# Queries of branch A's heads 2 and 3 moved from the projection stage into the gate steps, as a ninth pair of seven half-size products

## The chip, the cores and the metric

The kernel runs on one core of one Trainium2 chip. The metric is the device time of one execution in microseconds; the kernel before takes 1424.58 us (median of three executions, 1423.66 to 1425.17). The engines named below are PE (TensorE, the matrix unit; PEld is its loading of the stationary operand), DVE (VectorE), ACT (ScalarE), POOL (GpSimd) and SP (SyncE, which here issues almost all DMA transfers). Each works through its own stream of instructions in order, and semaphores tie the streams together.

## What is computed

One encoder block over 1024 tokens of width 1024, with 16 meta tokens in front of them that are dropped from the output. All data is float32. Cut to what matters here:

```python
proj = rms_norm(h, norm_mix) @ w_in        # qa, ka, va, qb, kb, vb, ga, gb side by side
y_a = differential_attention(qa, ka, va)   # 4 heads, two score maps each, all keys
y_b = windowed_gqa(qb, kb, vb, sink)       # 8 heads on 2 key heads, window 128
merged = sigmoid(ga) * (y_a @ w_ba) + sigmoid(gb) * (y_b @ w_bb)
h = h + merged @ w_o
h = h + swiglu(rms_norm(h, norm_ffn))
out = rms_norm(h, norm_final)
```

In branch A the queries `qa` of one head are 128 columns of `w_in`: twice 64, for the two score maps. Heads 2 and 3 are columns 256 to 511, side by side. Of `qa`, `ga` and `gb` only the rows of the 1024 tokens are used.

## The kernel before

**Precision.** [...] Each operand is split into a high part (a cast) and a low part (what the cast left), and a product is made of three: high by high, high by low, low by high. So a product of 128 output columns by 512 tokens over a depth of 1024 is 8 x 3 matmuls of 128 x 512; over a depth of 512 it is 4 x 3.

**Stage one: projections and branch B.** The normed tokens lie transposed in SBUF as `hT_hi` and `hT_lo`. `project_steps` (lines 219 to 234) projects 128 columns at a time; `order` (lines 204 to 209) lists the columns in the order in which their weights are loaded and split. `project_qa(h)` (lines 643 to 649) makes the queries of head h of branch A in two chunks of 512 tokens, 24 matmuls each; `evac_split` scales, splits and stages them, and they go to `qa_d[h]` in DRAM, high and low part in turn, for both maps. `project_kva(h)` makes values and keys. `units_b(g, qb)` runs branch B's attention, group g, over eight tiles of 128 queries. A tile (`attend_b`, lines 382 to 444) is a chain: scores on PE for four heads (line 397), bias and minimum on DVE (399), exponentials on ACT (403, 405), sum and reciprocal on DVE (406, 407), scaling on POOL (409), a copy of the meta columns on POOL (413), transposes on PE (422, 432), splits on ACT and DVE (425, 428, 434, 435), values on PE (429, 437), output on ACT and DVE (440, 441), store on SP (442). Two tiles may be under way; their transposes share two PSUM banks and their scores two more. In this stage a scheduler that plays the program through before the run sets the order on each engine; the projections that follow in the program are drawn in between the steps of B. On POOL `tokens_mixed` makes the sums of token blocks that the gates need, and keeps them in `t_d`.

**Stage two: branch A with gate steps between.** From line 1074 on PE's order is written out by hand. Branch A's attention runs over four heads of eight tiles, 32 in all. A tile has four score pieces ("s": `scores_a`, lines 959 to 996, which begins by needing the head's `aq` and `ak`), three transposes of the tile before ("t"), three parts of values or of the norm of earlier tiles ("n"), and gate steps ("g") between them. `SLOTS` (line 41) gives this order for a tile, `SLOTS_LAST` for what follows the last. `load_a(h)` queues the loads of a head's queries and keys when its first tile begins, followed by six gate steps (`G_HEAD`), 24 for head 0 (`G_FIRST`); two more stand before tile 1.

**The gates.** The 2048 gate columns are eight pairs of two blocks of 128 columns. A pair is a 2 x 2 product over halves (two column blocks, two token halves, two halves of the depth), and it is made by Winograd's scheme with seven products of half depth instead of eight: numbers p = 1, 2, 6, 5, 7, 3, 4, each 12 matmuls of 128 x 512, in four steps of three matmuls. Where p takes a sum of token blocks, that sum is loaded over a quarter of `hT_hi` and `hT_lo` (`turn_into`, lines 811 to 825), once all products that need the quarter as it was are done. So the products of all pairs run in two phases: `first_g` (lines 732 to 734) lists p = 1, 2, 6 of the eight pairs, then follow p = 5, 7, 3, 4 pair by pair (line 735). Between the phases a partial sum of each pair waits in DRAM (`u_d`) and is loaded back into `kept[k]` one or two products ahead of its use, where ACT copies it into a PSUM bank (lines 857 to 864).

`weights_g(n)` (lines 761 to 800) makes the operand of product n on POOL: sums of weight blocks (lines 777 to 790), then a cast and a subtraction (799, 800). Raw weights come through four buffers (`load_g`, lines 747 to 757; `n_freed` counts the buffers given back); operands have four places. `gate_steps` (lines 827 to 920) issues the products and takes the results out through tiles of the tag "g", of which there are three, and of the tag "u", of which there are four. Stores are collected in `held_stores` and issued on SP after head 0's values are queued.

Of the 224 steps, the last 22 (`HOLD`) are kept out of the slots and run after the last tile. What follows (projection of both branches from line 1268, output projection, feed-forward part) is made in the same way for both kernels.

## Time and profile before

| | before |
|---|---|
| median of three executions | 1424.58 us |
| the profiled execution | 1424.24 us |
| its span, first to last instruction | 1421.9 us |
| granted TensorE clock, mean | 0.998 |
| PE busy | 1401.0 us, 99% of the span |
| DVE, ACT, POOL busy | 64%, 47%, 45% |
| matmuls | 7183 |
| chain that ended last: PE's share | 90% |

How to read the views. A group of instructions has its source line, engine, operation, the tile it writes and the tiles it reads. The busy time of PE holds the whole duration of each matmul, and neighbouring matmuls overlap; the chain of waits has each piece once, so its pieces give the distance at which matmuls follow each other. In the chain a row is: start in us, length in us, engine, tile, line, and how many instructions. A timeline row is the same with shapes, and at its end in brackets the idle time before it and what ended it. A window row is: window and its length, then busy time and number of instructions of PE, PEld, DVE, ACT and POOL, the granted clock, the share of time in which the DMA engines were busy, and GB/s. A row of waits is: who waited, for whom, us in total, how often, the longest.

### The profile page before, as it was taken

How to read it: one execution, taken by the hardware profiler on the slowest of the kernel's cores; microseconds unless marked ns; L12 is line 12 of the kernel's file. 1: busy time of each engine (PE TensorE's matmuls, PEld its weight loads, DVE VectorE, ACT ScalarE, POOL GpSimd, SP SyncE). 2: the span in 40 equal slices, each digit the busy share in tenths (PEclk: the TensorE clock that was granted, in tenths of full speed). 3: DMA queues.
4: the chain of work that ended last, by engine and by line, in shares of the span. 5: the costliest groups of instructions: out<-in, count | busy, mean ns of one | idle time of the engine just before them, and what ended most of it. 6: DMA issues, size and time to landing. Idle time of an engine off the chain costs nothing.

```text
span 1421.9 us, 20667 instructions
## 1 busy us (share of the span) xinstructions
PE 1401.0 (99%) x7183; PEld 1202.7 (85%) x7183; DVE 914.8 (64%) x1584; ACT 672.1 (47%) x1284; POOL 636.7 (45%) x648
## 2 busy tenths in 40 slices
PE   9999999998999999999999999999999999999998
PEld 8998999987888888878888888888888888888886
DVE  6555666527787878666978956544555453787566
ACT  6355556435445555455346644333333333444454
POOL 4156865546677666322503055555545441000442
PEclk9999999999999999999999999999999999999999
DMA  8446565386896363296522724433333323954343
GB/s 235 92 128 184 154 199 160 106 290 225 259 318 211 105 209 105 68 342 198 149 103 90 207 90 148 148 106 98 101 111 104 97 97 110 353 186 144 120 128 144
DMA packets 194297, 228.27 MB, mean 161 GB/s; under 512 B 16824, under 2 KB 127360, under 8 KB 194192
## 3 DMA queue, kind: packets, MB, share of 16 engines
q1 hardware_dynamic: 192272, 224.11, 49.3%
q10 hardware_dynamic: 1920, 2.83, 0.7%
q8 instruction: 57, 0.93, 0.3%
q14 instruction: 48, 0.39, 0.1%
HBM read 152.48 MB, written 67.86 MB: 155 GB/s over the span
## 4 chain that ended last, share of the span: by engine, by line
PE 90%; DVE 4%; DMA 2%; ACT 1%; issue 1%; SPq 1%; POOL 1%; ACTq 0%; POOLq 0%; DVEq 0%
PE pg L1634 29%; PE pd L1738 14%; PE pg L881 8%; PE ppa L721 6%; PE po L1537 4%; PE pp_va L230 3%; PE pp_ka L230 3%; PE aps L977 3%; PE pp_qa L230 3%; PE apy L1019 3%; PE pp_qb L230 3%; PE bps L397 2%; PE po L1545 2%; PE bpy L437 1%; PE apt L1006 1%; PE bpt L432 1%
## 5 line engine op out<-in xcount | busy, mean ns | idle before, releaser
L1634 PE MATMUL pg<-t,wop 128*128 128x512 f32 x1056 | 242.5, 389 | 0.0
L1634 PEld LDWEIGHTS pg<-t,wop 128*128 128x128 f32 x1056 | 198.3, 188 | 41.1
L120 POOL TENSOR_TENSOR wop<-wf,wop 128x512 fp32r<-128x512 f32 x114 | 153.9, 1351 | 162.4 <-ACT wop L119 148.7
L1738 PE MATMUL pd<-ob,oa 128*128 128x512 f32 x924 | 210.1, 390 | 0.2 <-DVE ob L120 0.2
L1738 PEld LDWEIGHTS pd<-ob,oa 128*128 128x128 f32 x924 | 173.4, 188 | 36.8 <-DVE ob L120 1.0
L1634 PE MATMUL pg<-b,wop 128*128 128x512 f32 x792 | 183.3, 390 | 0.0
L1634 PEld LDWEIGHTS pg<-b,wop 128*128 128x128 f32 x792 | 148.5, 188 | 30.7
L881 PE MATMUL pg<-hT_hi,wopg 128*128 128x512 f32 x448 | 169.9, 400 | 2.7 <-POOL wopg L800 1.8
L119 ACT ACTIVATE wop<-wf 128x512 fp32r<-128x512 f32 x128 | 80.8, 633 | 73.4 <-PE pg L1634 44.3
L120 POOL TENSOR_TENSOR oa<-ra,oa 128x512 fp32r<-128x512 f32 x27 | 34.9, 1294 | 169.4 <-ACT oa L119 167.7
L119 ACT ACTIVATE oa<-ra 128x512 fp32r<-128x512 f32 x77 | 48.7, 632 | 109.0 <-PE pd L1738 50.8
L988 ACT ACTIVATE as<-as,amn 128x1040 f32<-128x1040 f32 x64 | 74.5, 1165 | 50.6 <-DVE amn L984 50.4
L881 PEld LDWEIGHTS pg<-hT_hi,wopg 128*128 128x128 f32 x448 | 84.3, 188 | 15.5 <-POOL wopg L800 2.2
L1411 DVE TENSOR_TENSOR s<-wf,wf 128x512 f32<-128x512 f32 x22 | 17.6, 798 | 112.2 <-DMA wf<-in_w_ff_up_dram 70.7
L977 PE MATMUL aps<-ak,aq 128*128 128x352 f32 (+1 forms) x384 | 86.6, 334 | 2.4 <-DVE amn L980 2.2
L881 PE MATMUL pg<-hT_lo,wopg 128*128 128x512 f32 x224 | 88.2, 394 | 0.0
L980 DVE CUSTOM_DVE_ANT_0 as<-aps,dist,far_a 128x704 f32<-128x704 f32 x64 | 60.3, 943 | 34.9 <-PE aps L977 34.6
L399 DVE CUSTOM_DVE_ANT_0 bs<-bps,tbx,nsink 128x432 f32<-128x432 f32 (+1 forms) x64 | 38.6, 629 | 61.6 <-PE bps L397 37.8
L1009 ACT ACTIVATE at<-apt 128x512 fp32r<-128x512 f32 (+1 forms) x96 | 45.4, 484 | 63.0 <-PE apt L1006 63.0
L977 PEld LDWEIGHTS aps<-ak,aq 128*128 128x128 f32 x384 | 64.2, 189 | 12.2 <-DVE amn L980 4.7
L409 POOL TENSOR_SCALAR bs<-bs,bdn 128x432 f32<-128x432 f32 (+1 forms) x64 | 36.9, 596 | 75.3 <-DVE bdn L407 34.4
L1019 PEld LDWEIGHTS apy<-at,av 128*128 128x128 f32 x400 | 54.2, 190 | 4.0
(321 smaller groups left out, 3131.1 us busy)
## 6 DMA issues: line engine op xcount, KB each, us to landing
ra<-aop SPq DMA_DIRECT2D x77, 256.0 KB, 2.7
wf<-in_w_ff_gate_dram SPq DMA_DIRECT2D x25, 512.0 KB, 3.8
wf<-in_w_ff_up_dram SPq DMA_DIRECT2D x25, 512.0 KB, 3.8
aop<-as SPq DMA_DIRECT2D x44, 256.0 KB, 2.1
w_c<-in_w_in_dram SPq DMA_DIRECT2D x17, 512.0 KB, 4.8
aop<-c SPq DMA_DIRECT2D x33, 256.0 KB, 2.0
ak<-ka_d SPq DMA_DIRECT2D x16, 520.0 KB, 6.5
t_d<-tst SPq DMA_DIRECT2D x16, 512.0 KB, 3.8
```

What stands on the lines that cost most here:

```text
L119: high = nc.scalar.activation(hi, src, AF.Copy)
L120: lo_eng.tensor_tensor(lo, src, f32(hi), ALU.subtract)
L230: product = nc.tensor.matmul(ps[:, :n], a[:, c, :], b[:, c, at:at + n], start=(u == 0), stop=(u == 3 * DC - 1))
L721: nc.tensor.matmul(ps, w[:, a, j, :], src(j, b, tk), start=(j == 0 and n == 0), stop=(j == 3 and n == 2))
L881: nc.tensor.matmul(ps, op[:, x, c, :], h[:, 4 * d + c, HALF[t]], start=(p in (1, 6, 7) and c == 0 and i == 0), stop=(p in (2, 6, 3, 4) and ...
L977: nc.tensor.matmul(ps[:, :n], qs[m][:, t * P:(t + 1) * P], ks[m][:, vv, k0:k0 + n], start=(vv == 0), stop=(vv == 1))
L980: nc.vector.tensor_tensor_reduce(s[m][:, 0:2 * n].rearrange("p (a k) -> p a k", a=2), two[:, :, :n], dist[:, u0:u0 + 2 * n].rearrange("p ( ...
L988: nc.scalar.activation(s[m][:, 0:L], s[m][:, 0:L], AF.Exp, bias=mn[:, m, 1:2], scale=-1.0, accum_out=dn[:, 1:2] if m else first_sum)
L1019: nc.tensor.matmul(py[:, cols], v[:kp, a, k, :], at_[:kp, k, b, :], start=(k == 0 and j == 0), stop=(k == 8))
L1537: nc.tensor.matmul(sets_o[p][u], oa[:, a, u * P:(u + 1) * P], ob[:, b, :], start=(p in (1, 5) and j == 0 and k == 0), stop=(p in (2, 3) an ...
L1634: nc.tensor.matmul(ps, op[:, x, c, :], b[:, y, c, :], start=(p in (1, 5) and c == 0 and n == 0), stop=(p in (4, 2, 3) and c == 3 and n == ...
L1738: nc.tensor.matmul(ps[u], oa[:, a, u * P:(u + 1) * P], ob[:, b, :], start=(p in (1, 2, 5) and j == 0 and k == 0), stop=(p in (2, 3, 4) and ...
```

## The change

`project_qa` is no longer called for heads 2 and 3, and their columns leave the list of weights of stage one. Instead the columns 256 to 511 become a ninth pair, `Q_PAIR` = 8, of the gate scheme: its products 1, 6 and 2 stand in the first phase ahead of the last gate pair, and it is the first pair of the second phase. A new function `keep_q` takes its four finished blocks out of PSUM: ACT scales and casts, DVE makes the low part, and four stores of 64 x 512 each go to `qa_d`. One block of `u_d` is added for its partial sum. The gate steps become 63 x 4 = 252 instead of 224. `SLOTS` becomes three strings: tiles of heads 0 and 1 alternate between one with six and one with seven gate steps, heads 2 and 3 keep five.

```diff
-SLOTS = "ssgsgntssgsgntgnt"
+SLOTS = "ssgsggntssgsgntgnt", "ssgsggntssgsggntgnt", "ssgsgntssgsgntgnt"
...
-    u_d = [dram.tile([P, 512], F32, name=f"u_d{i}") for i in range(8)]
+    u_d = [dram.tile([P, 512], F32, name=f"u_d{i}") for i in range(9)]
...
-        order += [C_QA + h * P]
+        order += [C_QA + h * P] if h < 2 else []
...
     for h in (2, 3):
-        all_of(project_qa(h))
         project_kva(h)
...
-    G_COLS = [C_GB + 2 * k * P for k in range(4)] + [C_GA + 2 * k * P for k in range(4)]
+    G_COLS = [C_GB + 2 * k * P for k in range(4)] + [C_GA + 2 * k * P for k in range(4)] + [C_QA + 2 * P]
+    Q_PAIR = 8
...
-    first_g += [(7, 1), (7, 2), (7, 6), (2, 6), (3, 6), (4, 6)]
-    order_g = first_g + [(k, p) for k in range(8) for p in (5, 7, 3, 4)]
+    first_g += [(Q_PAIR, 1), (Q_PAIR, 6), (Q_PAIR, 2), (7, 1), (7, 2), (7, 6), (2, 6), (3, 6), (4, 6)]
+    second_g = [Q_PAIR, *range(8)]
+    behind_g = dict(zip(second_g, second_g[1:]))
+    order_g = first_g + [(k, p) for k in second_g for p in (5, 7, 3, 4)]
...
-            n_freed[0] += 1 if k < 5 else 2 if k < 7 else 0
+            n_freed[0] += 1 if k < 5 else 2 if k != 7 else 0
...
+        def keep_q(total, block, t):
+            h = 2 + block
+            scale = -(2.0 ** (2 * h - 1))
+            hi, lo = (gstage.tile([P, 512], F32R, tag="g", name=f"{n}_{h}_{t}", bufs=G_BUFS) for n in ("qhi", "qlo"))
+            nc.scalar.activation(hi, total, AF.Copy, scale=scale)
+            nc.vector.scalar_tensor_tensor(lo, total, scale, f32(hi), ALU.mult, ALU.subtract)
+            for m in range(2):
+                for a, part in enumerate((hi, lo)):
+                    held_stores.append((qa_d[h][m, 64 * a:64 * a + 64, HALF[t]], f32(part)[64 * m:64 * m + 64]))
+            n_kept[0] += 1
...
-            k_next = {(5, 1): 0, (6, 1): 1, (7, 1): 2, (7, 6): 3, (2, 6): 4, (3, 6): 0}.get((k, p), k + 1 if p == 7 and k < 7 else None)
+            k_next = {(5, 1): 0, (6, 1): 1, (7, 1): 2, (7, 6): 3, (2, 6): 4, (3, 6): Q_PAIR}.get((k, p), behind_g.get(k) if p == 7 else None)
...
-            if n == n_first - 1 or (p == 4 and k < 7):
-                nxt = 0 if n < n_first else k + 1
+            if n == n_first - 1 or (p == 4 and k in behind_g):
+                nxt = second_g[0] if n < n_first else behind_g[k]
...
+                    elif k == Q_PAIR and p != 6 and p != 5:
+                        if p in (7, 4):
+                            total = kept.pop("q") if p == 7 else kept[k]
+                            add(total, ps, total, ALU.add)
+                        else:
+                            total = ps
+                        keep_q(total, int(p in (7, 4)), int(p in (7, 3)))
...
+                assert h < 2 or n_kept[0] == 4
...
-        for what in SLOTS if n < AH * NT else SLOTS_LAST:
+        for what in SLOTS[n % 2 if n < 2 * NT else 2] if n < AH * NT else SLOTS_LAST:
```

More of the change, by code (lines that the diff above doesn't have):

```diff
@@ L1046, in normed_a @@
         yield
+    n_kept = [0]
     gates = gate_steps()
```

## The prediction

> **What bounds the kernel now.** I read the page first, then the chain of waits in order of time, then the windows and the timelines around 195 to 340 us, where the change acts.

> ```profile
> span 1421.9 us, 20667 instructions
> PE 1401.0 (99%) x7183; PEld 1202.7 (85%) x7183; DVE 914.8 (64%) x1584; ACT 672.1 (47%) x1284; POOL 636.7 (45%) x648
> PE 90%; DVE 4%; DMA 2%; ACT 1%; issue 1%; SPq 1%; POOL 1%; ACTq 0%; POOLq 0%; DVEq 0%
> ```

> PE (TensorE) sets the time: it is busy for 99% of the span and carries 90% of the chain. So the first question is how many matmuls go. Their price is not the mean duration of the groups (390 ns, overlapping its neighbours) but the distance at which they follow each other, and the chain, which counts no overlap, shows that:

> ```profile
> 201.50 4.08 PE pp_qa L230 x18
> 291.34 0.23 PE bpy L437
> 291.93 1.75 PE pp_ka L230 x14
> 293.69 16.35 PE pg L881 x72
> 376.18 4.12 PE pg L881 x18
> 447.88 4.12 PE pg L881 x18
> 452.63 0.69 PE pg L881 x3
> 615.11 87.46 PE ppa L721 x384
> ```

> A 512-wide matmul of the projections costs 4.08/18 = 0.227 us, one of the gates 16.35/72 = 0.227 in a long row and 0.69/3 = 0.230 (0.695 a step) between other work. Stage one (projections and branch B) ends at 293.69, stage two (branch A with gate steps as filler) at 615.11. In stage one the last product of B (291.34) comes before the last 14 matmuls of the last key projection (291.93): B is covered to its end. The windows say the same; PE (first pair of numbers) has no gap from 195 to 294:

> ```profile
> 195.00:262.00 67.00, 67.00 (x379) 60.68 (x379) 40.68 (x107) 37.91 (x91) 39.71 (x42) 1.00 0.53 152
> 262.00:294.00 32.00, 32.00 (x209) 30.70 (x208) 15.89 (x36) 13.20 (x32) 12.40 (x23) 1.00 0.37 107
> 310.00:340.00 30.00, 27.14 (x150) 23.09 (x149) 20.93 (x52) 15.91 (x29) 14.77 (x19) 1.00 0.89 303
> ```

> **The change, part by part.** The sum is made against the profiled execution, 1424.24 us (span 1421.9 and 2.3 outside it); the median of the runs shown, 1424.58, lies 0.34 above it.

> *Removed from stage one:* the projections of heads 2 and 3, 2 x 48 matmuls of 512 columns: 96 x 0.227 = 21.8 us. Their four rounds of copies on ACT and DVE, two weight splits (ACT and POOL) and ten DMAs go too, beside PE.

> *Added to stage two:* seven products of 12 matmuls, 84, in 28 gate steps. The new slot strings hold 6 and 7 steps a tile instead of 5 over 16 tiles, 24 in all, and four are left for the end, so all of them stand between other work: 28 x 0.695 = +19.5 us. Counting PE alone the change is worth -2.3 us.

> *The cover that leaves.* B's second group is a chain of small steps through PE, DVE, ACT and POOL, and the removed matmuls were its filler. In the instruction order of the changed program the spacing of B's tiles against PE work hardly shrinks, so the projections now run out first. Its PE stream ends: 23 of 24 matmuls of the last key chunk, the values of tile 5, the last matmul, half of tile 7's scores, all transposes and values of tiles 6 and 7, and only then the 72 gate matmuls. PE's records of before stand in the order of its program, so the gates wait behind these values. Durations of the steps, most from tile 7 of before (the 288-column tile):

> ```profile
> 269.30 0.26 PE bps L397 x2
> 275.70 0.44 PE bpt L432 x4
> 270.05 0.52 DVE L399 CUSTOM_DVE_ANT_0 bs<-bps,tbx,nsink 128x288 f32<-128x288 f32 x1
> 270.17 0.54 ACT L403 ACTIVATE bs<-bs,bmn 128x288 f32<-128x288 f32 x1 [2.14 <-DVE bmn L399]
> 271.47 0.20 ACT L405 ACTIVATE bes<-bes 128x4 f32<-128x4 f32 x1
> 273.88 0.16 DVE L407 RECIPROCAL bdn<-bdn 128x4 f32<-128x4 f32 x1
> 274.24 1.95 POOL L409 TENSOR_SCALAR bs<-bs,bdn 128x288 f32<-128x288 f32 x4 [7.43 <-ACT vt_va L265]
> 276.25 0.29 POOL L413 COPY bmd<-bs 128x128 f32<-128x128 f32 x1
> 281.11 0.37 ACT L425 ACTIVATE bmh<-bpt,columns 128x128 fp32r<-128x128 f32 x1
> 281.79 1.42 DVE L428 SCALAR_TENSOR_TENSOR btm<-bpt,columns,bmh 32x128 fp32r<-32x128 f32 x4
> 286.73 0.60 ACT L434 ACTIVATE btr<-bpt 128x512 fp32r<-128x512 f32 x1 [1.84 <-PE bpt L432]
> 287.36 0.69 DVE L435 TENSOR_TENSOR btr<-bpt,btr 128x512 fp32r<-128x512 f32 x1 [1.88 <-ACT btr L434]
> 291.61 0.58 ACT L440 COPY by<-bpy 64x512 f32<-64x512 f32 x1 [0.98 <-PE bpy L437]
> ```

> From the start of tile 7's third score pair (0), each engine in its order: the scores end at 0.5; DVE first finishes a tile-5 split (0.69) and the last key chunk's, and is through the two L399 at 2.4; ACT runs two earlier exponentials, tile 6's L425, tile 5's L440, then this tile's third exponential, a tile-6 split and the fourth, to 4.55; tile 6's third transposes wait for a PSUM bank that DVE frees only after L428, so L405 ends at 5.35, and two small DVE steps end with L407 at 6.2; POOL L409 and L413 take 2.3 with the hand-overs, to 8.6. PE turns the meta columns and the first block (0.55) to 9.15; L425 and L428, behind tile 6's output addition, end at 10.75; PE turns the second block, whose bank was just freed, by 11.65; L434 to 12.45, L435 to 13.15, the last value at 13.4. In these 13.4 us PE has 4 scores, 15 values of 0.23 and 22 transposes of 0.11: 0.5 + 3.45 + 2.4 = 6.4. So PE stands for 7.0, and 0.3 more just before: +7.3 us. From below: the same steps without queues are 8.6 us, 2.2 of standing. From above: under its cover before, the way from the third score pair (269.30) to the last value (291.57) took 22.3, which would be 16. I take 7.3, since both the steps and their order are known.

> *The start of stage two.* The loads of weights and of head 0 stand on SP behind B's last output store; they went out at 297.52, 3.8 after the first gate matmul, and now the store leaves about 2 us after it. The first two gate operands are made on POOL before the tail. No cost, some 1.8 us of lead.

> *Heads 0 and 1.* PE's waits there, and what carried the largest of them:

> ```profile
> PE pg L881 <- POOL wopg L800: 1.8, 1, 1.8
> PE apt L1006 <- DVE at L1010: 1.7, 3, 0.8
> PE apt L1006 <- DVE adn L991: 1.0, 1, 1.0
> PE aps L977 <- DVE amn L980: 1.0, 3, 0.4
> PE pg L881 <- ACT p L887: 0.8, 1, 0.8
> 319.33 0.39 SPq L757 DMA_DIRECT2D wg_f<-in_w_in_dram  x1
> 334.12 1.28 POOL L777 TENSOR_TENSOR wg_m<-wg_m 128x512 f32<-128x512 f32 x1 [2.59 <-DMA wg_m<-in_w_in_dram]
> 337.55 1.28 POOL L800 TENSOR_TENSOR wopg<-wg_f,wopg 128x512 fp32r<-128x512 f32 x1
> ```

> The three rows on DVE, 3.7 us, are waits on the softmax; a denser filler gives DVE time, and I let it save 2.5 (ends 0 and 3.7). The wait on POOL grows: the operand of product (5, 6) is ready at 338.8, 45 us after the first gate matmul, because its weights come through DMA queues busy at 0.89 (the window 310 to 340) and POOL. It is gate step 44. Before, 24 + 5 + 2 + 5 + 5 + 3 steps reach it within tile 3; now 24 + 6 + 2 + 7 + 5 reach it at the end of tile 2, some 0.6 of a tile's other work (about 5 us) earlier, 3 us. Less part of the lead above: +2 (ends 0 and 4.5). What is behind it on PE is everything. The rest of the added work, seven splits and six sums on POOL (0.6 to 1.3 us each), four weight loads for two, 16 small query stores for 8, the partial sum's way out and back and one copy into PSUM on ACT, lies beside PE; its price, if the cover fails, is that same wait. The queries are complete at step 124; 136 steps are done when head 2's loads are queued, so they find them.

> *Sum:* -21.8 + 7.3 + 19.5 - 2.5 + 2 = +4.5. 1424.24 + 4.5 + 0.34 = 1429.0 us against the median. From the projection of the output on (615.11) the order of the instructions is unchanged.

> *A rule that would add to it.* The first matmuls of the run come slowly:

> ```profile
> 1.17 3.28 PE L497 MATMUL idle<-zeros 128*128 128x512 bf16 x8 [1.17 <-DVE zeros L489]
> 5.78 0.81 PE L510 MATMUL idle<-zeros 128*128 128x512 bf16 x3
> ```

> Eight take 3.28 (0.41 each), the later three lie 0.21 apart. If the tail's pauses brought that pace back for eight gate matmuls, it would be 8 x (0.41 - 0.227) = 1.5 us more: 1430.5. My longest single pause is about 1.6 us, so I give it little. [...]

> **The rivals.** (1) *The tail is short:* the engines overlap so well that PE stands 3 us or less. For it: nothing in the steps forbids 2.2. Against it: the order on ACT and DVE, which puts tile 6 between tile 7's steps. -21.8 + 3 + 19.5 - 2.5 + 2 = +0.2: 1424.8. (2) *Faster:* the added steps take over the stalls of heads 0 and 1, more than the wait view shows. From 293.69 to 447.88 + 4.12 us 158.3 us pass; summing the chain's paces over PE's order gives an estimate of 147, so 11 us are stalls. If 9 of them go (it decides from 7.3 on, with the tail as above and no later weights): -21.8 + 7.3 + 19.5 - 9 = -4.0: 1420.6. Against it: 2.6 of the listed waits are not on DVE, and the extra steps stand in only some of the gaps. (3) *The weights of head 0 decide:* +4.5 instead of +2 and nothing saved on DVE: +9.5, 1434.1. For it: DMA queues at 0.89 until 340. (4) *The queries come late:* head 2 waits for their stores. A store and a reload of this size land after 3.8 and 6.5 us:

> ```profile
> ak<-ka_d SPq DMA_DIRECT2D x16, 520.0 KB, 6.5
> t_d<-tst SPq DMA_DIRECT2D x16, 512.0 KB, 3.8
> ```

> 10.3 less the 4.1 of gate steps at the head's start (the row at 447.88) is +6 on the sum, 1435. Against it: 12 steps of lead, over 8 us.

> **How the numbers follow.** A measurement of this kernel tells about 0.2% (2.85 us) from no change: below 1421.7 is faster, above 1427.4 slower. Forecast and its near neighbours 0.53 (with the slow pace 0.05 of it); (1) 0.20; (2) 0.09; (3) 0.15; (4) 0.03. Faster 0.09; same: (1) and a little of the forecast's lower side, 0.24; slower 0.67. The ends of the unknown costs reach further (-3.8 to +18); leaving 2 in 10 outside, the range is 1423.5 to 1434.5, the forecast's own 1426 to 1432.

> **What would show it.** Right: the first gate matmul comes some 14.5 us earlier, near 279; the window before it shows PE partly empty, waiting for L428, L434, L435 and the transposes after L413; between that matmul and the first L721 some 340 us pass instead of 321; the wait on POOL L800 near gate step 44 is longer; waits on L980 and L1010 are fewer in the first 16 tiles. Wrong: PE without gaps up to the first gate matmul at 272 (the tail is hidden), or stage two longer by less than 15 us (the steps filled stalls) or more than 23.

## The result, and the profile after

The changed kernel takes 1431.16 us (median of 6 runs, 1430.77 to 1433.5), the kernel before 1424.26 in the runs beside it: 6.9 us more, a ratio of 1.0051 with a 95% interval of 1.0038 to 1.0063. The forecast was 1429.0 (+4.4), the range 1423.5 to 1434.5. So the direction and the size hold; the terms of the sum have to be looked at one by one, because not all of them hold.

The profiled execution of the changed kernel took 1433.5 us, the slowest of its six runs and 2.3 above their median. Its span is 9.8 us longer than that of the profiled run before, so stretches of this profile add up to more than the 6.9 us of the medians (10.5 us at the first output projection), and what is read from it below may be too large by some part of that. Its page begins so:

```profile
span 1431.7 us, 20669 instructions
PE 1406.9 (98%) x7171; PEld 1205.5 (84%) x7171; DVE 923.7 (65%) x1587; ACT 673.4 (47%) x1285; POOL 664.8 (46%) x666
PE 90%; DMA 4%; DVE 3%; ACT 1%; issue 1%; SPq 1%; POOL 1%; DVEq 0%; POOLq 0%; ACTq 0%
```

PE still sets the time, but with 12 matmuls fewer it is busy for 5.9 us more, and DMA has gone from 2% to 4% of the chain. The timeline of PE shows the end of branch B and the beginning of the gates (start, duration; in brackets the idle time before and what ended it):

```profile
265.24 0.97 PE L397 MATMUL bps<-kb,qb 128*128 128x288 f32 x4
...
276.83 0.77 PE L429 MATMUL bpy<-btm,vb 128*128 128x512 f32 x1 [1.64 <-DVE btm L428]
...
279.56 1.52 PE L437 MATMUL bpy<-btr,vb 128*128 128x512 f32 x2 [0.26 <-ACT btr L434]
282.47 0.80 PE L894 MATMUL pg<-hT_hi,wopg 128*128 128x512 f32 x1 [1.39 <-DVE by L441]
...
283.49 1.06 PE L894 MATMUL pg<-hT_hi,wopg 128*128 128x512 f32 x2
...
286.55 0.62 PE L894 MATMUL pg<-hT_hi,wopg 128*128 128x512 f32 x2
```

The first gate matmul starts at 282.47. In the timeline of the kernel before it starts at 293.52 (the chain, which counts no overlap, begins its piece at 293.69), so it comes 11.0 us earlier. The last value of B ends at 281.08, 15.8 us after the start of tile 7's third score pair, and the gates then wait 1.39 us more, for the addition of line 441. Two gate matmuls take 1.06 us at 283.5 and 0.62 three microseconds later. The windows put figures to the three stretches (PE's busy time first, the granted clock third from the end), those of the changed kernel above and stage two of the kernel before below:

```profile
195.00:262.00 67.00, 67.00 (x423) 64.50 (x423) 43.31 (x108) 38.03 (x92) 43.08 (x49) 1.00 0.47 145
262.00:282.47 20.47, 14.09 (x62) 8.88 (x60) 11.83 (x31) 9.01 (x22) 7.56 (x18) 0.83 0.25 61
282.47:625.57 343.10, 333.49 (x1924) 294.01 (x1925) 235.96 (x510) 164.76 (x301) 227.56 (x246) 0.99 0.61 202
```

```profile
293.52:615.11 321.59, 310.69 (x1843) 274.28 (x1841) 227.31 (x505) 159.15 (x293) 199.91 (x232) 1.00 0.61 203
```

PE has no gap up to 262, then it stands for 6.4 of 20.5 us. Stage two, from the first gate matmul to the first output projection, takes 343.1 us, 21.5 more. In it PE stands for 9.6 us instead of 10.9: the 21.5 us are all in busy time, 22.8 us of it, where 28 steps of 0.695 explain 19.5. For the other 3.3 there are stretches at half clock, 9.9 us of them in this stage; if PE did half as much in them as at full clock, they cost 4.9 us (an estimate, half of the 9.9), so they are enough for it, but no run takes them away alone. Windows of 3.4 us around the three places where it falls:

```profile
268.50:271.90 3.40, 2.37 (x13) 1.64 (x13) 3.15 (x9) 2.06 (x8) 0.00 (x0) 1.00 0.47 111
271.90:275.30 3.40, 2.10 (x9) 0.90 (x7) 1.43 (x3) 1.58 (x4) 3.18 (x11) 1.00 0.03 8
275.30:278.70 3.40, 1.87 (x7) 1.60 (x7) 2.03 (x5) 0.52 (x1) 3.32 (x9) 0.51 0.17 39
278.70:282.10 3.40, 2.12 (x4) 0.67 (x3) 1.06 (x2) 1.18 (x2) 1.06 (x1) 0.50 0.00 0
282.10:285.50 3.40, 3.03 (x7) 2.48 (x8) 0.32 (x1) 0.00 (x0) 0.00 (x0) 0.50 0.35 83
285.50:288.90 3.40, 3.40 (x16) 2.73 (x16) 0.00 (x0) 0.59 (x1) 1.26 (x2) 0.98 1.15 363
...
323.10:326.50 3.40, 0.81 (x3) 0.38 (x3) 2.38 (x3) 1.64 (x4) 3.40 (x5) 1.00 0.11 22
326.50:329.90 3.40, 3.40 (x11) 2.93 (x12) 2.20 (x4) 0.28 (x1) 2.91 (x4) 0.51 0.87 245
...
408.40:411.80 3.40, 1.17 (x6) 0.80 (x5) 3.12 (x8) 0.18 (x1) 3.40 (x4) 1.00 1.05 393
411.80:415.20 3.40, 3.40 (x14) 2.97 (x13) 0.49 (x2) 1.67 (x3) 3.40 (x4) 0.52 1.04 386
```

Each time a window with PE busy for 0.8 to 2.1 us is followed by one at half clock, in the second and third place although PE then works all through it; after 2.4 us (the first row) the clock stays. What PE waits for in stage two, with the first gate matmul (us in total, times, longest):

```profile
PE pg L894 <- DVE u L918: 2.2, 1, 2.2
PE pg L894 <- POOL wopg L802: 2.1, 1, 2.1
...
PE pg L894 <- DVE by L441: 1.4, 1, 1.4
PE pg L894 <- DMA hT_hi<-t_d: 1.2, 1, 1.2
PE aps L997 <- DVE amn L1000: 1.0, 3, 0.4
PE pg L894 <- ACT p L900: 0.9, 2, 0.5
PE apt L1026 <- DVE at L1030: 0.9, 1, 0.9
...
PE pg L894 <- POOL wopg L801: 0.6, 1, 0.6
...
PE apt L1026 <- DVE adn L1011: 0.3, 1, 0.3
PE pg L894 <- DVE g L925: 0.3, 1, 0.3
```

The softmax rows (lines 997 and 1026) are down to 2.2 us, and only the 0.3 on line 1011 lies in heads 0 and 1. In their place stand waits of the gates: for their weights (802 and 801), for the sum of line 918, and for the turned tokens.

### The profile page after: what moved, and what is told of

Its sections match the earlier page's. It is cut to its first block, busy times and chain, and to the rows that moved or that the text cites. A ratio compares the mean times of both kernels' runs of the same rounds, so it can differ in the third digit from the quotient of the medians.

```text
span 1431.7 us, 20669 instructions
## 1 busy us (share of the span) xinstructions
PE 1406.9 (98%) x7171; PEld 1205.5 (84%) x7171; DVE 923.7 (65%) x1587; ACT 673.4 (47%) x1285; POOL 664.8 (46%) x666
## 4 chain that ended last, share of the span: by engine, by line
PE 90%; DMA 4%; DVE 3%; ACT 1%; issue 1%; SPq 1%; POOL 1%; DVEq 0%; POOLq 0%; ACTq 0%
PE pg L1656 29%; PE pd L1760 14%; PE pg L894 8%; PE ppa L720 6%; PE po L1559 4%; PE aps L997 3%; PE pp_ka L230 3%; PE pp_va L230 3%; PE pp_qb L230 3%; PE apy L1039 3%; PE apt L1026 2%; PE bps L397 2%; PE pp_qa L230 2%; PE po L1567 2%; PE bpy L437 1%; PE bpt L432 1%
## 5 line engine op out<-in xcount | busy, mean ns | idle before, releaser
L894 PE MATMUL pg<-hT_hi,wopg 128*128 128x512 f32 x504 | 190.7, 405 | 8.8 <-DVE u L918 2.2
L894 PEld LDWEIGHTS pg<-hT_hi,wopg 128*128 128x128 f32 x504 | 96.0, 191 | 26.0 <-issue 2.9
L894 PE MATMUL pg<-hT_lo,wopg 128*128 128x512 f32 x252 | 100.0, 397 | 0.0
L399 DVE CUSTOM_DVE_ANT_0 bs<-bps,tbx,nsink 128x432 f32<-128x432 f32 (+1 forms) x64 | 38.7, 628 | 58.1 <-PE bps L397 36.6
L997 PEld LDWEIGHTS aps<-ak,aq 128*128 128x128 f32 x384 | 65.5, 192 | 10.2 <-DVE amn L1000 2.2
L409 POOL TENSOR_SCALAR bs<-bs,bdn 128x432 f32<-128x432 f32 (+1 forms) x64 | 37.2, 600 | 69.1 <-DVE bdn L407 29.5
## 6 DMA issues: line engine op xcount, KB each, us to landing
wf<-in_w_ff_gate_dram SPq DMA_DIRECT2D x25, 512.0 KB, 3.9
wf<-in_w_ff_up_dram SPq DMA_DIRECT2D x25, 512.0 KB, 3.8
wg_s<-in_w_in_dram SPq DMA_DIRECT2D x18, 512.0 KB, 4.4
t_d<-tst SPq DMA_DIRECT2D x16, 512.0 KB, 3.3
```

What stands on the lines that cost most here:

```text
L894: nc.tensor.matmul(ps, op[:, x, c, :], h[:, 4 * d + c, HALF[t]], start=(p in (1, 6, 7) and c == 0 and i == 0), stop=(p in (2, 6, 3, 4) and ...
L997: nc.tensor.matmul(ps[:, :n], qs[m][:, t * P:(t + 1) * P], ks[m][:, vv, k0:k0 + n], start=(vv == 0), stop=(vv == 1))
```

## The experiments

Ratios are to the kernel before, measured beside each. The start of the first gate matmul and of the first output projection are from the profile of each kernel.

| kernel | median us | ratio, 95% interval | first gate | first output projection |
|---|---|---|---|---|
| before | 1424.3 | | 293.5 | 615.1 |
| changed | 1431.2 | 1.0051 (1.0038 to 1.0063) | 282.5 | 625.6 |
| e1, stage one alone | 1412.5 | 0.9923 (0.9911 to 0.9936) | 284.5 | 610.4 |
| e2, stage two alone | 1450.3 | 1.0180 (1.0167 to 1.0193) | 293.5 | 642.8 |
| e3, pauses filled | 1430.1 | 1.0042 (1.0030 to 1.0054) | 281.3 | 624.1 |
| e4, another bank | 1432.1 | 1.0058 (1.0045 to 1.0070) | 280.9 | 624.4 |
| e5, key projection held | 1432.3 | 1.0048 (1.0033 to 1.0063) | 280.7 | 625.7 |
| e6, steps moved back | 1441.1 | 1.0111 (1.0094 to 1.0128) | 283.2 | 633.4 |
| e7, e5 and e6 | 1437.5 | 1.0087 (1.0071 to 1.0103) | 279.6 | 628.4 |
| e8, e2 and e6 | 1448.8 | 1.0166 (1.0151 to 1.0181) | 292.9 | 641.1 |
| e9, loads on POOL | 1563.6 | 1.0975 (1.0957 to 1.0993) | 289.4 | 758.3 |
| e10, e2 with loads on POOL | 1590.7 | 1.1172 (1.1153 to 1.1191) | 308.0 | 784.0 |
| e11, stores on ACT | 1436.6 | 1.0081 (1.0068 to 1.0095) | 284.2 | 629.3 |
| e12, e3, e4 and e11 | 1431.9 | 1.0056 (1.0044 to 1.0069) | 279.7 | 623.5 |

The profiled run of e1 took 1418.05, 5.5 more than its median; its two starts belong to that run. Stage two takes some 326 us in it, with the same work for which the kernel before takes 321.6, so this profile doesn't tell where the time of its median went.

### The two halves of the change

e1 takes the projections out of the kernel before; heads 2 and 3 then read the queries of heads 0 and 1:

```diff
-        order += [C_QA + h * P]
+        order += [C_QA + h * P] if h < 2 else []
...
-        all_of(project_qa(h))
...
-                nc.sync.dma_start(f32(q), qa_d[h][m])
+                nc.sync.dma_start(f32(q), qa_d[h % 2][m])
```

> The kernel before with the projections of the queries of heads 2 and 3 taken out of stage one and nothing put in their place: these two heads read the queries of heads 0 and 1, so their projection isn't computed; stage two does the same work as before. Theory A, the terms of the prediction (96 matmuls gone, 21.8 us, of which 7.3 us come back as waiting in branch B's last tiles): 14.5 us less than before, about 1409.8. Theory B, the profile of the changed kernel (its first gate matmul stands 10.7 us earlier within the stage, with the PSUM bank of B's output held until the line 441 and the granted clock at 0.50 to 0.55 for some 10 us added to the waiting): about 11 us less, 1413.3. Rival, the projections were no cover at all: 21.8 us less, 1402.5.

It saved 11.8 us, which is nearer to theory B, and a loss of 10.0 of the 21.8 us of matmuls. e2 puts the projections back into the changed kernel and stores the ninth pair elsewhere:

```diff
-                    held_stores.append((qa_d[h][m, 64 * a:64 * a + 64, HALF[t]], f32(part)[64 * m:64 * m + 64]))
+                    held_stores.append((qx_d[block][m, 64 * a:64 * a + 64, HALF[t]], f32(part)[64 * m:64 * m + 64]))
...
-        order += [C_QA + h * P] if h < 2 else []
+        order += [C_QA + h * P]
...
+        all_of(project_qa(h))
```

> The changed kernel with the projections of all four heads back in stage one; the ninth pair is still computed beside the gates, but its stores go to a spare buffer, so that the queries are computed twice. B's last tiles have their cover again, and the time above the kernel before is what the ninth pair costs in stage two. Theory A, the terms of the prediction (19.5 for 28 steps, less 2.5 of softmax waits, and 2 for late operands): 19.0 us more than before, 1443.3. Theory B, the profile of the changed kernel (343.3 us from the first gate matmul to the first output projection instead of 321.4, with two stretches of some 3.4 us at half clock in it): up to 21.8 us more, 1446.1. If stage two alone takes under 15 us more, 1439 or less, the steps fill waits of PE and the loss lies in B's last tiles.

It cost 26.0 us, more than either theory said. The halves add up to +14.2, the change to +6.9: they aren't independent, and together they cost 7.3 us less than apart. The waits of e2 in stage two (its lines 803 and 804 are 801 and 802 of the changed kernel), its loads of weights on SP's queue, and two windows in which the clock falls here too (0.87 and 0.83):

```profile
PE pg L896 <- POOL wopg L803: 5.2, 1, 5.2
PE pg L896 <- POOL wopg L804: 2.1, 2, 1.6
PE pg L896 <- POOL wg_s L793: 2.0, 1, 2.0
```

```profile
297.51 1.21 SPq L761 DMA_DIRECT2D wg_f<-in_w_in_dram  x2
...
319.35 0.38 SPq L761 DMA_DIRECT2D wg_f<-in_w_in_dram  x1
```

```profile
320.00:340.00 20.00, 12.88 (x66) 10.18 (x65) 10.40 (x23) 9.00 (x16) 9.77 (x12) 0.87 0.79 267
420.00:440.00 20.00, 17.51 (x88) 14.73 (x87) 12.96 (x30) 5.95 (x11) 13.86 (x16) 0.83 1.05 368
```

The same loads in the changed kernel:

```profile
283.11 1.27 SPq L759 DMA_DIRECT2D wg_f<-in_w_in_dram  x2
...
304.86 0.38 SPq L759 DMA_DIRECT2D wg_f<-in_w_in_dram  x1
```

With its cover back, B ends when PE ends, and the loads follow 4.0 us behind the first gate matmul; in the changed kernel, where PE stands while B ends, they follow 0.6 behind, and the later pair 22.4 instead of 25.8. e2 waits 9.3 us for POOL's operands, the changed kernel 2.7; the difference of 6.6 is most of the 7.3. That suggests that a microsecond in which PE stands at the end of B is in part a microsecond in which it doesn't wait for weights later. It is a reading of two profiles; no run shows it alone.

### The end of branch B

e3 lays matmuls that nobody reads into the pauses of B's last two tiles, in a bank of the scores:

```diff
+            warm = bank(psum1, "bs", f"warm_{nm}", 2) if g and t > 5 else None
+            def keep_warm(behind, n, w, x, to):
+                with tc.issue_after(behind.ins):
+                    for _ in range(n if warm is not None else 0):
+                        nc.tensor.matmul(warm[:, :to], w, x, start=True, stop=True)
...
+                keep_warm(mm, 6 if k == b0 else 0, vb[g][:, 0, :], hT_hi[:, 0, 0:512], 512)
...
+                keep_warm(mm, 6 if t == 7 and k == b1 - 1 else 1, vb[g][:, 0, :], hT_hi[:, 0, 0:512], 512)
```

> The changed kernel with some 20 matmuls of 0.23 us, whose product nobody reads, laid into the waits of PE in B's last two tiles, in a free PSUM bank. Theory A, the granted clock falls to 0.50 there because PE is idle in so much of a stretch of some 3 us, and that costs time of its own: the clock stays at 1.00 up to the first gate matmuls, these stand 0.23 us apart instead of 0.43 (1.5 us), and the products and transposes of the last tile run faster: 2 to 3 us less than the changed kernel, about 1428.8. Rival, the waits alone cost the time and the low clock comes along with them for nothing: the same as the changed kernel, 1431.2, or up to 1 us more for matmuls that stand in the way.

Its windows of PE:

```profile
272.00:276.00 4.00, 3.51 (x17) 2.11 (x16) 2.03 (x5) 2.14 (x4) 3.86 (x14) 1.00 0.01 3
276.00:280.00 4.00, 3.30 (x15) 1.94 (x14) 2.06 (x4) 0.68 (x2) 3.69 (x5) 1.00 0.14 33
280.00:284.00 4.00, 3.99 (x18) 2.95 (x17) 0.68 (x1) 0.50 (x1) 0.00 (x0) 1.00 0.24 56
```

The clock stayed at 1.00 with PE busy for 10.8 of these 12 us, and these matmuls are all that was added: in the changed kernel, where PE is busy for 6.1 of the 10.2 us from 271.9 to 282.1, it fell because PE had too little to do there. The first gate matmul came 1.2 us earlier, and the median is 1.1 us lower. The intervals of the two ratios overlap, so the gain on the whole time is not settled; it is less than the 2 to 3 us expected.

e4 gives the first gate product a bank of its own:

```diff
+    bank(psum2, "acc", "acc_first", 1)
```

> The changed kernel with one more PSUM tile named ahead of the first gate product, so that this product doesn't get the bank of branch B's output, which is held until the copy and the addition of lines 440 and 441 have read it. Theory A, this bank is what the first gate matmul waits for in the end (1.4 us): it starts 1.2 to 1.4 us earlier, and the time is 0.7 to 1.4 us less than that of the changed kernel, 1429.8 to 1430.5. Rival, the first gate matmul meets another wait at the same place, or the gain is lost again in the wait for the operand of product (5, 6): the same as the changed kernel.

The first gate matmul started 1.5 us earlier, at 280.94, without a wait: the bank was what it waited for. The time did not fall (1432.1), as its rival had it. PE's timeline shows a new wait on the way and the old one behind it:

```profile
280.94 0.63 PE L895 MATMUL pg<-hT_hi,wopg 128*128 128x512 f32 x1
...
317.74 0.73 PE L895 MATMUL pg<-hT_hi,wopg 128*128 128x512 f32 x2 [1.02 <-POOL wopg L803]
...
324.98 0.80 PE L895 MATMUL pg<-hT_hi,wopg 128*128 128x512 f32 x1 [2.12 <-POOL wopg L803]
```

e5 orders the last key projection behind B's last score matmul, as cover (`HELD_K` is 1, and `scored_b` holds that matmul):

```diff
-        project(C_KA + h * P, K_CHUNKS, f"ka{h}", evac_split(None, k_consume))
+        for i, _ in enumerate(steps := project_slowly(C_KA + h * P, K_CHUNKS, f"ka{h}", evac_split(None, k_consume))):
+            if h == AH - 1 and i >= HELD_K - 1:
+                with tc.issue_after(scored_b[0].ins):
+                    all_of(steps)
```

> The changed kernel with all but the first three of the 72 matmuls of head 3's key projection ordered on PE behind the last score matmul of branch B, so that they lie in the waits of B's last tiles. Theory L, covered tail but late weights: the tail's 11 us of waiting go and the first gate matmul starts at 271 to 273 us, but the raw weights of the gates are loaded behind the last stores of stage one, as in the run that projected the queries twice, so that product (5, 6) and its neighbours wait for their operands some 9 us, as they did there, where the changed kernel waits 2.7 us: 2 to 5 us less than the changed kernel, 1426 to 1429. Rival C, the cover is all that is missing: 10 to 11 us less, 1420.5. Rival N, held matmuls delay B's last tiles as much as they fill: the same as the changed kernel, 1431.

Theory L expected 1426 to 1429 and rival N no change: no change it was, but not in N's way. Two windows of e5:

```profile
245.00:262.00 17.00, 13.88 (x61) 10.55 (x60) 12.39 (x34) 9.74 (x28) 11.51 (x16) 0.80 0.15 47
262.00:280.70 18.70, 17.30 (x113) 15.82 (x111) 11.37 (x26) 8.57 (x20) 6.34 (x17) 1.00 0.50 142
```

The last stretch is covered now (1.4 us idle instead of 6.4), but the matmuls are missed before it, where PE stands for 3.1 us and the clock falls to 0.80. B's chain as a whole has too little work beside it. The 1.8 us by which the gates start earlier are gone by the first output projection (625.65 against 625.57).

### The weights at the start of stage two

e6 moves gate steps from the first three tiles to later ones:

```diff
-        for what in SLOTS[n % 2 if n < 2 * NT else 2] if n < AH * NT else SLOTS_LAST:
+        for what in SLOTS[3 if n < 3 else 1 if n < 2 * NT else 2] if n < AH * NT else SLOTS_LAST:
```

The first three tiles take a new string with four steps, the tiles 3 to 15 have seven, which is one step fewer in all than before the edit.

> The changed kernel with four gate steps in each of the first three tiles of scores instead of six, seven and six, and seven in each of the tiles 3 to 15 (so that the queries are ready in time as before). Theory L, the operand of product (5, 6) comes late because its raw weights land late, and is missed 2.7 us and some 1.5 us more by a stretch at half clock: with seven steps fewer ahead of it that wait is gone, 2 to 4 us less than the changed kernel, 1427 to 1429. Rival, the softmax waits of the first tiles, which the added steps had filled, come back or the wait moves to the next product: 1430.5 or more.

It lost 10 us against the changed kernel. Its waits in stage two:

```profile
PE pg L894 <- POOL wopg L802: 5.6, 1, 5.6
PE apt L1026 <- DVE at L1030: 4.5, 4, 2.0
PE apt L1026 <- DVE as L1014: 2.7, 2, 2.1
```

The wait near step 44 is gone, as theory L has it. The softmax waits are back, as the rival has it, and a weight is waited for later, 5.6 us at 422.6. In this kernel the even filling is worth more than the wait near step 44 that goes with it. e7 and e8 put the same slots into e5 and e2:

> Both of the two edits above in the changed kernel: key projection of head 3 held back as cover, and fewer gate steps in the first three tiles. Theory L: the tail is covered and the weights are in time, so that the change shows what it saves on PE and in softmax waits (21.8 less 19.5, and some 2.5): 1419 to 1422, under the kernel before. Rival C (cover alone decides) gives about 1420 both here and for the covered one without the slots. If the weights are late still, 1426 or more.

> The kernel that projects the queries twice (1450.3 us), with four gate steps in each of the first three tiles and seven in the tiles 3 to 15. Theory L: of its 26 us over the kernel before, some 9 are waits for operands whose raw weights land late and 1 to 2 the half clock behind them; they go with the later demand: 1440 to 1443, which is the 17 to 19 us that the prediction gave stage two. Rival, the 26 us are in the steps themselves: 1448 or more.

Theory L missed in both (1437.5 and 1448.8). e8 came out where its rival had it, though not by the steps alone: a weight is still waited for in one place (5.5 us), and the softmax waits are over 6 us. e7 lies in the range kept for late weights, but its view has no wait for POOL's operands; it has 8.5 us of softmax waits and one gate step that waits 5.4 us for something that the view doesn't name. Fewer steps at the start made two kernels slower (e6 and e7) and left the third (e8 beside e2) within 1.5 us.

e9 and e10 let POOL issue the loads of weights, in two halves:

```diff
-                raws_g.append(nc.sync.dma_start(w, w_in[:, col:col + P].rearrange("(c p) n -> p c n", p=P)))
+                for half in (slice(0, 4), slice(4, 8)):
+                    last = nc.gpsimd.dma_start(w[:, half], w_in[:, col:col + P].rearrange("(c p) n -> p c n", p=P)[:, half])
+                raws_g.append(last)
```

> The changed kernel with the loads of the gates' raw weights issued by POOL, in two halves each, instead of SP, so that they don't stand behind the stores and the loads of head 0 in SP's queue. Theory L, SP's queue makes the operand of product (5, 6) late (in the changed kernel the second load of a pair is issued 22.4 us after the first gate matmul, the operand is ready 43.9 us after it): PE's waits for the operands of lines 801 and 802 (2.7 us) go, and the half clock behind them (1.6 us): 2 to 4 us less than the changed kernel, 1427 to 1429. Rival, POOL itself or the landing of the transfers sets when the operand is ready: the same wait, and the time that POOL takes to issue comes on top: 1431 to 1436.

> The kernel that projects the queries twice (1450.3 us) with the loads of the gates' raw weights issued by POOL in two halves instead of SP. There B's last tiles have their cover, the first load of gate weights is issued 4.0 us after the first gate matmul instead of 0.6, and PE waits 9.3 us for POOL's operands. Theory L: these waits and the half clock go, 8 to 10 us less, 1440 to 1443, so that stage two costs what the prediction gave it, 17 to 19 us. Rival, the operands are late whoever issues the loads, or the 26 us are in the steps: 1448 or more.

They took 132 and 140 us more than the kernels that they were made from. e9 is far outside both of its theories; e10 lies in its rival's range only because that has no upper end. One row of POOL's groups and one of PE's waits of e9:

```profile
L760 POOL DMA_DIRECT2D wg_s<-in_w_in_dram x36 | 27.7, 770 | 78.0 <-issue 76.1 <-POOL wopg L803 1.0 <-POOL as L1017 0.6
```

```profile
PE pg L896 <- POOL wopg L804: 85.3, 21, 10.6
```

Each issue takes POOL 0.77 us and POOL stands 2.2 us before it on average (78.0/36), and its other work comes behind. That tells nothing of SP's queue. It does show how directly PE hangs on the supply of weights.

e11 lets ACT issue the output stores of B's last two tiles, behind which the loads stood on SP:

```diff
-            nc.sync.dma_start(yb_d[g][:, t * P:(t + 1) * P].rearrange("(r d) t -> d r t", r=4),
+            (nc.scalar if g and t > 5 else nc.sync).dma_start(yb_d[g][:, t * P:(t + 1) * P].rearrange("(r d) t -> d r t", r=4),
```

> The changed kernel with the stores of branch B's last two tiles (line 442) issued by ACT instead of SP. In the changed kernel the loads of the third and fourth raw weight and of head 0's queries and keys stand in SP's queue behind the last of these stores (282.4 us), though SP is idle from 270. Theory L, that queue makes the operands of the first products late: the two loads are issued at 271 to 272, PE's waits for the operands of lines 801 and 802 (2.7 us) and the stretch at half clock behind them (1.6 us) go or shrink: 2 to 4 us less than the changed kernel, 1427 to 1429. Rival, the loads wait for memory that stage one holds until its end, or the later loads wait for POOL to free their buffers: the same as the changed kernel, 1430.5 to 1432.

SP's queue in e11:

```profile
272.11 1.25 SPq L759 DMA_DIRECT2D wg_f<-in_w_in_dram  x2
...
282.84 0.81 SPq L965 DMA_DIRECT2D ak<-ka_d  x2
...
292.25 0.38 SPq L759 DMA_DIRECT2D wg_f<-in_w_in_dram  x1
```

The first two loads left 11 us earlier. The keys of head 0 then held up the queue until 282.84, when B ends, and the third load left at 292.25, 3.6 us later than in the changed kernel (288.61). The kernel got 5.5 us slower, outside both expectations. What holds the keys the trace doesn't name; that their memory is B's until then is likely, and was not tried.

e12 joins e3 (with no matmul behind the last value), e4 and e11:

> The changed kernel with three edits together: the stores of B's last two tiles on ACT's queue, matmuls that nobody reads in the waits of these tiles (none behind the last value), and a bank of its own for the first gate product. If the terms add, the first gate matmul starts at about 280 at full clock, and the operands of the first products are in time: 1.1 us (as measured for the filled waits), 1.4 us for the bank and 2 to 4 us for the loads, 1424.5 to 1427, level with the kernel before at best. If the gain of an earlier start is taken back by late operands, as with the bank alone: 1429 to 1431.

The gates started at 279.66, 2.8 us earlier, at full clock. The median is 1431.9, the changed kernel's again and a little above the second expectation. Its waits:

```profile
PE pg L903 <- DVE u L927: 3.8, 1, 3.8
PE pg L903 <- POOL wopg L811: 3.6, 3, 1.8
```

They are the changed kernel's 2.2 and 2.7, each grown; the 1.2 for the turned tokens is gone. Four kernels (e3, e4, e5, e12) started the gates 1.2 to 2.8 us earlier, and none was measurably faster for it. No kernel that projects all queries beat the kernel before.

## Why the prediction came out

*Removed, 21.8 us.* No run shows this term alone. e1 gives what was left of it, 11.8 us.

*The cover that leaves, +7.3.* Right in its place and its order, too small: 10.0 by e1, 10.8 in the profile (21.8 less 11.0). Up to the first gate matmul PE stands for 8.4 us instead of 2.9 and is busy for 274.0 instead of 290.6. So only 5.5 us of the loss are added standing. The other 5.2 are longer work: 16.6 us of busy time went, not 21.8, because a matmul of 512 columns that doesn't overlap its neighbour counts with all of its duration (0.39 us for a gate product at full clock, 0.63 at half, in the timeline), and my sum had the values at their pace of 0.23. From tile 7's third score pair to the end of the last value 15.8 us passed instead of 13.4. With the pauses filled (e12) that way takes 14.7 us (265.13 to 279.82), so some 1.2 of the 2.4 went with the half clock; the rest is in my steps. And the step behind the last value was missing: the first gate product gets the bank of B's output, and waits for its copy and addition (lines 440 and 441), 1.39 us, as e4 showed by taking that wait away. 13.4 + 2.4 + 1.4 makes 17.2, which is 282.47 less 265.24.

*Added, 28 steps, +19.5.* No run measures it alone. PE's busy time grew by 22.8 us in stage two. By heads: 24 of the steps lie in heads 0 and 1 (up to the gate steps at the start of head 2, at 458.89 in the changed kernel and 447.88 in the kernel before), where it grew by 20.9 us for 16.7 forecast, and all stretches at half clock lie there too. In heads 2 and 3 it grew by 1.9 for the 2.8 of four steps.

*Heads 0 and 1, -2.5.* Inside its ends of 0 and 3.7: of the 3.7 us of softmax waits in these heads 0.3 are left, 3.4 less. I had not counted on heads 2 and 3, where they fell as well, from 3.6 to 1.9, so that the whole stage has 5.0 less (7.2 to 2.2).

*Late operands, +2.* The wait that I named grew by less: 43.9 us after the first gate matmul product (5, 6) waits 2.1 us, and a product three microseconds before 0.6, together 2.7 instead of 1.8, so +0.9. The lead that I gave as 1.8 was 3.4 (the loads leave 0.6 instead of 4.0 us behind the first gate matmul). What I had missed is a second place at 408 to 424, where the first round of products runs out ahead of its sums and of the turned tokens (2.2 and 1.2). All late operands together go from 2.6 us (1.8 + 0.8) to 7.3, 4.7 more. So the size of this term came out too small, and by another wait than mine. With the softmax waits of the whole stage the two terms make -0.3 against -0.5 forecast; that they nearly cancel is luck.

*What would have added to it.* I gave the half clock 0.05, because my longest single pause was 1.6 us; that the length of a single pause decides was my assumption, which no run shows. The pauses were that short (1.72 us at most in B's tail, 2.2 later), and the clock fell to 0.50, three times. The gates' first matmuls came 0.43 us apart, the pace that I had costed at 1.5 us. In B's tail no single pause explains it: the kernel before has one of 1.76 us (up to 338.89), and its clock stays at 1.00. In the changed kernel, how full a stretch of 3.4 us is goes with it better: at full clock 62%, 24% and 34% busy were followed by half clock and 70% was not, and at half clock 55% and 62% did not end it. (3.4 us is how long two of its stretches at half clock lasted, 326.5 to 329.9 and 411.8 to 415.2; the first, 275.3 to 285.5, lasted 10.2.) That share alone doesn't decide either: in the kernel before PE was busy for 51% of such a stretch (1.73 us, 335.4 to 338.8), and the next one had full clock. By what measure of PE's work the clock falls, no run shows.

*The rivals.* (1), the short tail, is out: PE stands for 6.4 us in it. (2), stalls filled, is out: in heads 0 and 1 PE stood for only 6.3 us before (154.4 us, 148.1 of them busy), not the 11 that I had estimated, and 3.4 of its 9 us were saved. (3), the weights of head 0, is out too: the wait for them grew by 0.9 us, not 4.5, and DVE's saving, which it denied, came along; the 4.7 us of all late operands reach its size by other waits. (4), late queries: no such wait is in the view.

*The marks.* The first gate matmul near 279 (282.5), stage two some 340 us (343.1, 21.5 more, under the 23 that I had set as wrong), PE partly empty behind L428, L434, L435 and L413, a longer wait near step 44 (2.7 for 1.8), and fewer on the softmax all appeared.

The sum assumed that the terms add. e1 and e2 show that they don't: apart they make +14.2. Too low by 2.7 us in the first half (-14.5 forecast) and by 7 in the second (+19.0), it would have missed each half alone by more than it missed the whole, 2.5. Both errors point the same way; what made up for them is the 7.3 us that the halves cost less together, which no term of the sum holds. That the total came so near is luck. The reason that the profiles suggest is the head start that the standing at B's end gives the loads (0.6 against 4.0 us behind the first gate matmul). A clean test, weights early and nothing else changed, was not reached: e9 and e11 each brought a larger cost of their own.

## What to carry to other kernels

Work that is taken away from one stage was also the cover of the chain beside it: walk that chain to the release of the last bank that the next stage takes (1.39 us of waiting here), and don't count as won what the next stage loses again in waiting for its own loads. Where a chain of short waits would leave PE busy for about as little as here (2.1 of 3.4 us, with no pause over 1.72), count the half clock in as possible. And test the halves of a change apart: a sum can be right with both halves wrong.
